# Attention scores of one head in one three-bank PSUM tile, with one maximum and one exponential

## The chip, the cores and the metric

The kernel runs on one core of a Trainium2 chip. The metric is the device time of one execution in microseconds (us). Each kernel is run several times, and the median is given. A difference of less than about 0.2% (7 us here) can't be told from no change.

## The reference

Two layers of a hybrid backbone run over 256 context tokens and 1024 latent tokens of width 1024. Each layer mixes the tokens by three groups of heads that share one input projection (attention, a gated recurrence in both directions, a Fourier transform), joins them by an output projection, and then applies a gated feed-forward part with a convolution. The change touches attention alone:

```python
def attend(q, k, v):
    s = jnp.einsum('bhgqd,bhkd->bhgqk', q, k).astype(jnp.float32) * (HEAD_DIM ** -0.5)
    p = jax.nn.softmax(s, axis=-1).astype(v.dtype)
    return jnp.einsum('bhgqk,bhkd->bhgqd', p, v)
```

There are 8 query heads of 64 channels and 2 key/value heads. A latent query sees all 1280 keys (256 of the context, 1024 latent), in both layers. A context query sees the 256 context keys, and is needed in layer 0 only.

## The kernel before, in words

**Tiles and units.** Queries go in tiles of 128 tokens: 2 of the context, 8 latent. A unit of `attention` is one tile and one pair of heads, so layer 0 has 8 units of the context and 32 latent ones, and layer 1 has 32 latent ones. In heads that is 16 of the context and 64 latent ones in layer 0, and 64 latent ones in layer 1: 144 in all.

**`score` (L545 to L590).** For each head of a unit the keys are cut into segments of at most 512, which gives 512, 512 and 256 for a latent head and one of 256 for a context head. Each segment has a PSUM tile of one bank, with the tag `s` and three buffers (L564). Two matmuls fill it (L566 and L567: queries against the low and high parts of the keys), VectorE takes its maximum over the keys (L569), and a second, small reduction joins the segments' maxima and negates them (L572). ScalarE then takes the exponential of each segment (L576) into an SBUF tile `p`, and adds up the rows into `su`. At a tile's last pair the sums are added over the segments (L584) and inverted (L585).

**`value` (L592 to L625).** For each two key blocks, TensorE transposes four 128x128 pieces of `p` into a one-bank tile `ps_t` (L602, two buffers), ScalarE copies out a rounded part `ph` (L607), VectorE the rest `pl` (L608), and four matmuls with the values add into `ps_o` (L612 and L614). A unit has five such steps for latent queries.

**PSUM.** While attention runs, the pool holds eight banks: three `s`, two `g` (projections, Fourier and others), one `o`, two `pt`.

**What sets the order.** L627 to L641 run the values of a unit in turns with the scores of the next one. `interleave` (L649) mixes attention with three other pieces of work, in this order: the rest of the input projection (`project_rest`: tiles `pxs` and `pws`, lines 158 to 160), the Fourier part, and the recurrence (tiles such as `psc`, `W`, `tot`). The table `LACE` holds the shares. A scheduler then orders each engine's instructions when the program is built, with its own estimates of durations; `ahead` (L107, table `AHEAD`) raises the priority of the named steps by a number per layer. On the chip each engine runs its instructions strictly in that order, and waits in it.

Of the kernel before, what the change touches and what calls it, by code (L numbers as in the profile page):

```python
# [11 lines left out]
F32 = mybir.dt.float32  # L12
# [47 lines left out]
QT_PAIRS = 1  # L60
QT_BUFS = 3
IN_WP = 2
P_BUFS = {512: 10, 256: 5}

C_Q, C_KV, C_HQ, C_HI, C_FF, C_FB, C_HG, C_FT = 0, 512, 768, 1024, 1280, 1536, 1792, 2048

# [30 lines left out]
def hybrid_backbone_kernel(ctx: ExitStack, tc: tile.TileContext, A: dict, out: bass.AP):  # L97
# [439 lines left out]
    def attention(l, S, ap, psn, finished):  # L537
# [6 lines left out]

        def score(i, pr):  # L545
            nk = keys(i)
            segs = [(s, min(512, nk * P - s)) for s in range(0, nk * P, 512)]
            ns = len(segs)
            if pr == 0:
                su = ap.tile([P, NH, 3], F32, tag="su", bufs=2, name="su")  # L550
                state["su", i] = su
            su = state["su", i]
            if pr % QT_PAIRS == 0:
                nh = 2 * QT_PAIRS
                state["qt"] = ap.tile([P, nh, P], F32R, tag="qt", bufs=QT_BUFS, name="qt")
                nc.gpsimd.dma_start(out=state["qt"], in_=S["QT"][i][:, 2 * pr:2 * pr + nh, :])  # L556
            qt = state["qt"]
            kv = pr // 2
            ps2 = []
            for h in (2 * pr, 2 * pr + 1):  # L560
                mx = ap.tile([P, 4], F32, tag="mx", bufs=4, name="mx")
                sc, p = [], []
                for j, (s0, n) in enumerate(segs):
                    t = psn.tile([P, 512], F32, tag="s", bufs=3, name="ps_s")  # L564
                    with ahead("qk" if (i, pr) != units[0] else "pt"):
                        nc.tensor.matmul(t[:, 0:n], lhsT=qt[:, h % (2 * QT_PAIRS), :], rhs=KT[:, 2 * kv + 1, s0:s0 + n], start=True, stop=False)  # L566
                        nc.tensor.matmul(t[:, 0:n], lhsT=qt[:, h % (2 * QT_PAIRS), :], rhs=KT[:, 2 * kv, s0:s0 + n], start=False, stop=True)  # L567
                    with ahead("max"):
                        nc.vector.tensor_reduce(out=mx[:, j:j + 1], in_=t[:, 0:n], axis=AX.X, op=ALU.max)  # L569
                    sc.append(t)  # L570
                with ahead("max"):
                    nc.vector.tensor_reduce(out=mx[:, 3:4], in_=mx[:, 0:ns], axis=AX.X, op=ALU.max, negate=True)  # L572
                for j, (s0, n) in enumerate(segs):
                    t = ap.tile([P, n], F32, tag=f"p{n}", bufs=P_BUFS[n], name="p")
                    with ahead("exp"):
                        nc.scalar.activation(out=t, in_=sc[j][:, 0:n], func=AF.Exp, bias=mx[:, 3:4],  # L576
                                             accum_out=su[:, h, j:j + 1])
                    p += [t[:, c:c + P] for c in range(0, n, P)]
                ps2.append(p)
                yield 0.84e-3 * nk * P  # L580
            state["p", i, pr] = ps2
            if pr == NH // 2 - 1:
                rs = ap.tile([P, NH], F32, tag="rs", bufs=2, name="rs")
                nc.vector.tensor_reduce(out=rs, in_=su[:, :, 0:ns], axis=AX.X, op=ALU.add)  # L584
                nc.vector.reciprocal(out=rs, in_=rs)  # L585
                t = psn.tile([P, 512], F32, tag="g", bufs=2, name="ps_rs")
                nc.tensor.transpose(t[0:NH, 0:P], in_=rs, identity=ident)
                rt = ap.tile([NH, P], F32, tag="rst", bufs=2, name="rst")
                nc.vector.tensor_copy(rt, t[0:NH, 0:P])
                nc.sync.dma_start(out=S["rs"][:, i * P:(i + 1) * P], in_=rt)  # L590
# [1226 lines left out]
```

## Time and profile before

| | us |
|---|---|
| median of 3 runs | 3408.84 |
| the runs | 3407.70 to 3414.72 |
| the profiled execution's own time | 3419.26 |
| its span, first to last instruction | 3417.4 |

The profile is of one execution. PE is TensorE's matmuls, PEld its loads of weights (the stationary operand), DVE is VectorE, ACT ScalarE, POOL GpSimd. The profiled execution is 10.4 us above the median, and 1.9 us of it lie outside the span. Attention runs from 284 to about 800 us in layer 0, and from 2060 to 2515 us in layer 1. In each layer it stands beside the input projection first (to about 500 and 2300 us), and beside Fourier and recurrence after that. A matmul's busy time in the profile is longer than the distance from its start to that of the next one, since they are pipelined.

### The profile page before, as it was taken

How to read it: one execution, taken by the hardware profiler on the slowest of the kernel's cores; microseconds unless marked ns; L12 is line 12 of the kernel's file. 1: busy time of each engine (PE TensorE's matmuls, PEld its weight loads, DVE VectorE, ACT ScalarE, POOL GpSimd, SP SyncE). 2: the span in 40 equal slices, each digit the busy share in tenths (PEclk: the TensorE clock that was granted, in tenths of full speed). 3: DMA queues.
4: the chain of work that ended last, by engine and by line, in shares of the span. 5: the costliest groups of instructions: out<-in, count | busy, mean ns of one | idle time of the engine just before them, and what ended most of it. 6: DMA issues, size and time to landing. Idle time of an engine off the chain costs nothing.

```text
span 3417.4 us, 55716 instructions
## 1 busy us (share of the span) xinstructions
PE 3116.8 (91%) x20897; PEld 2540.3 (74%) x20897; DVE 2417.0 (71%) x4171; ACT 1550.2 (45%) x3105; POOL 1261.6 (37%) x1134
## 2 busy tenths in 40 slices
PE   6999998989889999798899999998978889998896
PEld 4879976778766777576798888876766668776675
DVE  4614568887698888547876755668877798886568
ACT  4325556664443433233465435655642434443332
POOL 3522105422464444241235341115435545553323
PEclk9999999999989999899999999998998899999898
DMA  7643122117764443698775432122035642225993
GB/s 214 204 153 85 49 93 58 40 44 220 224 183 142 129 129 122 192 246 205 242 209 178 131 105 70 47 90 65 21 112 159 195 130 74 79 81 159 255 227 123
DMA packets 457412, 468.60 MB, mean 137 GB/s; under 512 B 32244, under 2 KB 343989, under 8 KB 457143
## 3 DMA queue, kind: packets, MB, share of 16 engines
q1 hardware_dynamic: 422294, 409.24, 37.9%
q0 software_dynamic: 34848, 55.80, 8.6%
q8 instruction: 165, 2.70, 0.3%
q14 instruction: 105, 0.85, 0.1%
HBM read 370.41 MB, written 94.54 MB: 136 GB/s over the span
## 4 chain that ended last, share of the span: by engine, by line
PE 28%; DVE 16%; DMA 14%; issue 9%; POOL 9%; ACT 3%; SPq 0%; POOLq 0%; DVEq 0%; ACTq 0%
PE pu L158 4%; POOL wlo L1217 4%; PE pu L159 4%; PE pu L160 4%; DMA araw<-act 3%; DMA X<-in_w_down_dram 3%; DVE cv L1105 3%; DMA raw<-in_w_down_dram 2%; PE ps_t L602 2%; PE ps_s L566 1%; DVE wlo L1348 1%; PE ps_o L612 1%; DVE U L1232 1%; DMA hraw<-yT 1%; DVE S L1204 1%
## 5 line engine op out<-in xcount | busy, mean ns | idle before, releaser
L1217 POOL TENSOR_TENSOR wlo<-S,whi 128x512 fp32r<-128x512 f32 x176 | 283.0, 1618 | 281.9 <-ACT whi L1216 268.2
L1105 DVE SCALAR_TENSOR_TENSOR cv<-U,cw,cv 128x512 f32<-128x512 f32 x352 | 326.0, 974 | 33.9 <-ACT cv L1102 33.8
L158 PE MATMUL pd<-whi,wlo 128*128 128x512 f32 x616 | 248.5, 411 | 58.5 <-DVE wlo L1348 50.2
L569 DVE TENSOR_REDUCE mx<-ps_s 128x1 f32<-128x512 f32 (+1 forms) x400 | 222.2, 588 | 108.0 <-PE ps_s L567 106.9
L608 DVE TENSOR_TENSOR pl<-ps_t,ph 128x512 fp32r<-128x512 f32 x328 | 223.0, 686 | 86.2 <-ACT ph L607 84.1
L145 POOL TENSOR_TENSOR wlo<-raw,whi 128x1024 fp32r<-128x1024 f32 x69 | 168.1, 2438 | 298.6 <-ACT whi L144 298.5
L602 PE MATMUL ps_t<-ident,p 128*128 128x128 f32 x1312 | 263.1, 284 | 13.6 <-DVE pl L608 8.1
L159 PE MATMUL pd<-wlo,whi 128*128 128x512 f32 x616 | 250.9, 407 | 17.5 <-DVE wlo L1348 14.3
L576 ACT ACTIVATE p<-ps_s,mx 128x512 f32<-128x512 f32 (+1 forms) x400 | 243.2, 617 | 52.0 <-DVE mx L572 42.3
L607 ACT CAST ph<-ps_t 128x512 fp32r<-128x512 f32 x328 | 190.9, 589 | 162.3 <-PE ps_o L614 80.4
L1102 ACT ACTIVATE cv<-U,cb,cw 128x512 f32<-128x512 f32 x176 | 137.6, 815 | 258.1 <-DVE U L1232 210.5
L160 PE MATMUL pd<-whi 128*128 128x512 f32 x616 | 249.2, 405 | 0.0
L158 PE MATMUL pxs<-whi,hlo 128*128 128x256 f32 x752 | 221.5, 295 | 5.8 <-DVE hraw L1524 4.3
L159 PE MATMUL pxs<-wlo,hhi 128*128 128x256 f32 x752 | 216.5, 288 | 0.5 <-DVE wlo L145 0.4
L160 PE MATMUL pxs<-whi,hhi 128*128 128x256 f32 x752 | 216.4, 288 | 0.0
L612 PE MATMUL ps_o<-pl,V 128*128 128x256 f32 x656 | 201.1, 323 | 6.7 <-DVE pl L608 4.8
L1217 POOL TENSOR_TENSOR wlo<-raw,whi 128x512 fp32r<-128x512 f32 x108 | 149.7, 1392 | 129.8 <-ACT whi L1216 115.6
L602 PEld LDWEIGHTS ps_t<-ident,p 128*128 128x128 f32 x1312 | 165.1, 143 | 36.8 <-DVE pl L608 10.9
L158 PEld LDWEIGHTS pd<-whi,wlo 128*128 128x128 f32 x616 | 119.3, 195 | 94.1 <-DVE wlo L1348 56.2
L1232 DVE TENSOR_TENSOR U<-pu,U 128x512 f32<-128x512 f32 x252 | 167.4, 686 | 26.9 <-PE pu L160 18.5
L614 PE MATMUL ps_o<-ph,V 128*128 128x256 f32 x656 | 183.2, 297 | 0.0
L556 POOL DMA_DIRECT2D qt<-QT x72 | 40.5, 563 | 374.6 <-PE ps_s L567 277.1
(395 smaller groups left out, 9423.6 us busy)
## 6 DMA issues: line engine op xcount, KB each, us to landing
raw<-in_w_up_dram SPq DMA_DIRECT2D x144, 512.0 KB
raw<-in_w_ada_dram SPq DMA_DIRECT2D x96, 512.0 KB
raw<-in_w_down_dram SPq DMA_DIRECT2D x62, 512.0 KB
act<-cv SPq DMA_DIRECT2D x88, 256.0 KB
araw<-act SPq DMA_DIRECT2D x40, 512.0 KB
raw<-in_w_in_dram SPq DMA_DIRECT2D x36, 512.0 KB
X<-in_w_down_dram POOLq DMA_DIRECT2D x30, 512.0 KB, 17.2
Y<-act POOLq DMA_DIRECT2D x30, 512.0 KB, 17.8
```

The costliest lines, as they stand in the source:

```text
L158: nc.tensor.matmul(o, lhsT=al, rhs=bh, start=start, stop=False)
L159: nc.tensor.matmul(o, lhsT=ah, rhs=bl, start=False, stop=False)
L160: nc.tensor.matmul(o, lhsT=ah, rhs=bh, start=False, stop=stop)
L569: nc.vector.tensor_reduce(out=mx[:, j:j + 1], in_=t[:, 0:n], axis=AX.X, op=ALU.max)
L576: nc.scalar.activation(out=t, in_=sc[j][:, 0:n], func=AF.Exp, bias=mx[:, 3:4], accum_out=su[:, h, j:j + 1])
L602: nc.tensor.transpose(t[:, ss, h, :], in_=ps2[h][2 * s2 + ss], identity=ident)
L607: nc.scalar.copy(ph, tv)
L608: nc.vector.tensor_tensor(out=pl, in0=tv, in1=f32(ph), op=ALU.subtract)
L612: nc.tensor.matmul(o, lhsT=V[:, s, kv, 1:3, :].rearrange("p a c -> p (a c)"), rhs=pl[:, ss, :], start=(s == 0), stop=False)
L1105: nc.vector.scalar_tensor_tensor(out=o, in0=u[:, tap:tap + n], scalar=convw[l][tap][:, c:c + 1], in1=o, op0=ALU.mult, op1=ALU.add)
L1217: nc.gpsimd.tensor_tensor(out=lo, in0=src, in1=f32(hi), op=ALU.subtract)
L1232: nc.vector.tensor_tensor(out=o, in0=x, in1=y, op=op)
```

## The change

A head's scores lie in one PSUM tile of three banks (1536 elements, of which 1280 or 256 are used), with one buffer. All six matmuls of a latent head write into it, each into a single bank. One reduction takes the negated maximum over all keys, and one exponential is written to a `p` tile of 1280 elements, of which there are five. The row sum comes from that exponential alone, so the small reductions of L572 and L584 are gone. PSUM use stays at eight banks, and the SBUF of `p` stays the same (10 x 512 + 5 x 256 = 5 x 1280). `LACE` and `AHEAD` stay as they were.

```diff
-P_BUFS = {512: 10, 256: 5}
+P_BUFS = 5
...
-                su = ap.tile([P, NH, 3], F32, tag="su", bufs=2, name="su")
+                su = ap.tile([P, NH], F32, tag="su", bufs=2, name="su")
...
-                mx = ap.tile([P, 4], F32, tag="mx", bufs=4, name="mx")
-                sc, p = [], []
-                for j, (s0, n) in enumerate(segs):
-                    t = psn.tile([P, 512], F32, tag="s", bufs=3, name="ps_s")
+                mx = ap.tile([P, 1], F32, tag="mx", bufs=4, name="mx")
+                t = psn.tile([P, 3 * 512], F32, tag="s", bufs=1, name="ps_s")
+                for s0 in range(0, n, 512):
+                    sl = slice(s0, min(n, s0 + 512))
                     with ahead("qk" if (i, pr) != units[0] else "pt"):
-                        nc.tensor.matmul(t[:, 0:n], lhsT=qt[:, h % (2 * QT_PAIRS), :], rhs=KT[:, 2 * kv + 1, s0:s0 + n], start=True, stop=False)
-                        nc.tensor.matmul(t[:, 0:n], lhsT=qt[:, h % (2 * QT_PAIRS), :], rhs=KT[:, 2 * kv, s0:s0 + n], start=False, stop=True)
-                    with ahead("max"):
-                        nc.vector.tensor_reduce(out=mx[:, j:j + 1], in_=t[:, 0:n], axis=AX.X, op=ALU.max)
-                    sc.append(t)
+                        nc.tensor.matmul(t[:, sl], lhsT=qt[:, h % (2 * QT_PAIRS), :], rhs=KT[:, 2 * kv + 1, sl], start=True, stop=False)
+                        nc.tensor.matmul(t[:, sl], lhsT=qt[:, h % (2 * QT_PAIRS), :], rhs=KT[:, 2 * kv, sl], start=False, stop=True)
                 with ahead("max"):
-                    nc.vector.tensor_reduce(out=mx[:, 3:4], in_=mx[:, 0:ns], axis=AX.X, op=ALU.max, negate=True)
-                for j, (s0, n) in enumerate(segs):
-                    t = ap.tile([P, n], F32, tag=f"p{n}", bufs=P_BUFS[n], name="p")
-                    with ahead("exp"):
-                        nc.scalar.activation(out=t, in_=sc[j][:, 0:n], func=AF.Exp, bias=mx[:, 3:4],
-                                             accum_out=su[:, h, j:j + 1])
-                    p += [t[:, c:c + P] for c in range(0, n, P)]
+                    nc.vector.tensor_reduce(out=mx, in_=t[:, 0:n], axis=AX.X, op=ALU.max, negate=True)
+                e = ap.tile([P, NT * P], F32, tag="p", bufs=P_BUFS, name="p")
+                with ahead("exp"):
+                    nc.scalar.activation(out=e[:, 0:n], in_=t[:, 0:n], func=AF.Exp, bias=mx, accum_out=su[:, h:h + 1])
+                p = [e[:, c:c + P] for c in range(0, n, P)]
...
-                nc.vector.tensor_reduce(out=rs, in_=su[:, :, 0:ns], axis=AX.X, op=ALU.add)
-                nc.vector.reciprocal(out=rs, in_=rs)
+                nc.vector.reciprocal(out=rs, in_=su)
```

The change also moves instructions, since the scheduler orders the whole program again. Outside the two attention stretches the order on TensorE is the same. In the changed kernel L566 and L567 are still the score matmuls and L569 is the maximum; the transposes are L596, the split L602, the value matmuls L606 and L608, the reciprocal L579, and `ob` L614.

On TensorE in layer 1, beside the input projection, the order before has this. A head's three score tiles (`ps_s`, six matmuls) are written as the banks come free, here the first one ahead of two value matmuls and the others behind them:

```order
9292 L612 MATMUL ps_o<-pl,V 128x256
9293 L614 MATMUL ps_o<-ph,V 128x256
9294 L566 MATMUL ps_s<-KT,qt 128x512
9295 L567 MATMUL ps_s<-KT,qt 128x512
9296 L612 MATMUL ps_o<-pl,V 128x256
9297 L614 MATMUL ps_o<-ph,V 128x256
9298 L566 MATMUL ps_s<-KT,qt 128x512
9299 L567 MATMUL ps_s<-KT,qt 128x512
9300 L566 MATMUL ps_s<-KT,qt 128x256
9301 L567 MATMUL ps_s<-KT,qt 128x256
9302 L612 MATMUL ps_o<-pl,V 128x256
```

In the order of the change the six stand together, and behind them come other matmuls up to the next head's six. The previous head's last score matmul here is number 9405; from 9406 to 9427 stand 9 value matmuls, 11 projection matmuls and 6 transposes, whose end is shown:

```order
9421 L158 MATMUL pxs<-whi,hlo_18244 128x256
9422 L159 MATMUL pxs<-wlo,hhi_18243 128x256
9423 L606 MATMUL ps_o<-pl,V 128x256
9424 L608 MATMUL ps_o<-ph,V 128x256
9425 L606 MATMUL ps_o<-pl,V 128x256
9426 L608 MATMUL ps_o<-ph,V 128x256
9427 L596 MATMUL ps_t<-ident,p 128x128 x2
9428 L566 MATMUL ps_s<-KT,qt 128x512
9429 L567 MATMUL ps_s<-KT,qt 128x512
9430 L566 MATMUL ps_s<-KT,qt 128x512
9431 L567 MATMUL ps_s<-KT,qt 128x512
9432 L566 MATMUL ps_s<-KT,qt 128x256
```

The score matmuls of a head moved together, and the distance to the next head's became one stretch of other work.

On VectorE at about the same place, the order before has the three maxima and the small one (`mx`) between the splits (`pl`):

```order
2224 L608 TENSOR_TENSOR pl<-ps_t,ph 128x512 x2
2225 L569 TENSOR_REDUCE mx<-ps_s 128x1 x3
2226 L608 TENSOR_TENSOR pl<-ps_t,ph 128x512
2227 L572 TENSOR_REDUCE mx<-mx 128x1
2228 L608 TENSOR_TENSOR pl<-ps_t,ph 128x512
2229 L589 COPY rst<-ps_rs 8x128
```

In the order of the change one reduction stands for the four, between two splits each time:

```order
2055 L602 TENSOR_TENSOR pl<-ps_t,ph 128x512 x2
2056 L569 TENSOR_REDUCE mx<-ps_s 128x1
2057 L602 TENSOR_TENSOR pl<-ps_t,ph 128x512
2058 L583 COPY rst<-ps_rs 8x128
2059 L602 TENSOR_TENSOR pl<-ps_t,ph 128x512
```

A split that could slip in between the maxima of a head now stands before or behind one longer reduction.

## Rows read from the trace of the kernel before

**Rows 1.** The page: each engine's busy time, share of the span and instructions.
```profile
PE 3116.8 (91%) x20897; PEld 2540.3 (74%) x20897; DVE 2417.0 (71%) x4171; ACT 1550.2 (45%) x3105; POOL 1261.6 (37%) x1134
```

**Rows 2.** Stretches: start:end, length, busy (x count) of PE, PEld, DVE, ACT, POOL; PEclk.
```profile
284.00:500.00 216.00, 212.59 (x1452) 186.69 (x1453) 123.93 (x289) 124.45 (x326) 26.77 (x30) 0.99 0.26 78
500.00:800.00 300.00, 272.88 (x3813) 222.40 (x3812) 239.81 (x584) 193.37 (x506) 112.32 (x155) 0.95 0.24 68
2060.00:2300.00 240.00, 237.78 (x1567) 201.67 (x1566) 145.16 (x303) 146.40 (x372) 30.74 (x35) 1.00 0.23 68
2300.00:2515.00 215.00, 192.48 (x2891) 156.83 (x2890) 174.14 (x410) 132.61 (x357) 88.34 (x112) 0.94 0.14 39
```

**Rows 3.** Stretches of the score tile alone: busy (x count) of PE, PEld, DVE, ACT.
```profile
500.00:800.00 300.00, 65.67 (x211) 35.01 (x210) 59.50 (x108) 71.90 (x216) 0.95 0.24 68
...
2300.00:2515.00 215.00, 43.00 (x144) 24.00 (x144) 41.36 (x72) 50.42 (x150) 0.94 0.14 39
```

**Rows 4.** Groups by line and shape, VectorE: count | busy, mean ns | idle before.
```profile
L608 DVE TENSOR_TENSOR pl<-ps_t,ph 128x512 fp32r<-128x512 f32 x328 | 223.0, 686 | 86.2 <-ACT ph L607 84.1
L569 DVE TENSOR_REDUCE mx<-ps_s 128x1 f32<-128x512 f32 x256 | 171.3, 685 | 76.2 <-PE ps_s L567 75.5
...
L569 DVE TENSOR_REDUCE mx<-ps_s 128x1 f32<-128x256 f32 x144 | 59.7, 416 | 31.8 <-PE ps_s L567 31.4
...
L572 DVE TENSOR_REDUCE mx<-mx 128x1 f32<-128x3 f32 x128 | 19.0, 149 | 1.2
```

**Rows 5.** Groups by line and shape, ScalarE, same columns.
```profile
L607 ACT CAST ph<-ps_t 128x512 fp32r<-128x512 f32 x328 | 190.9, 589 | 162.3 <-PE ps_o L614 80.4 <-PE ps_t L602 72.2 <-DVE pl L608 3.5
L576 ACT ACTIVATE p<-ps_s,mx 128x512 f32<-128x512 f32 x256 | 176.0, 692 | 39.5 <-DVE mx L572 38.6
...
L576 ACT ACTIVATION_READ_ACCUMULATOR p<-ps_s,mx 128x1 f32 x400 | 82.2, 206 | 0.0
L576 ACT ACTIVATE p<-ps_s,mx 128x256 f32<-128x256 f32 x144 | 69.3, 482 | 12.5 <-PE ps_t L602 8.3 <-DVE mx L572 3.7
```

**Rows 6.** Line L566 (first score matmul): its engine sat idle until (us, times).
```profile
  ACT p L576: 25.2, 88
```

**Rows 7.** Lines L602 (transposes) and L612 (first value matmul): idle until (us, times).
```profile
  DVE pl L608: 18.9, 22
...
  ACT p L576: 4.9, 12
...
  DVE pl L608: 13.4, 22
```

**Rows 8.** Timeline of TensorE in layer 1: start, us, line and operation, count.
```profile
2155.34 0.28 PE L612 MATMUL ps_o<-pl,V 128*128 128x256 f32 x1
2155.45 0.28 PE L614 MATMUL ps_o<-ph,V 128*128 128x256 f32 x1
...
2156.28 0.39 PE L566 MATMUL ps_s<-KT,qt 128*128 128x512 f32 x1
2156.51 0.39 PE L567 MATMUL ps_s<-KT,qt 128*128 128x512 f32 x1
...
2158.74 0.60 PE L602 MATMUL ps_t<-ident,p 128*128 128x128 f32 x4
2159.10 0.36 PE L158 MATMUL pxs<-whi,hlo 128*128 128x256 f32 x1
...
2331.85 0.76 PE L773 MATMUL psc<-q,kc 64*32 64x32 f32 x64
```

**Rows 9.** Timelines of VectorE and ScalarE in layer 0, one handover from maximum to exponential.
```profile
427.20 0.16 DVE L572 TENSOR_REDUCE mx<-mx 128x1 f32<-128x3 f32 x1
...
427.39 0.69 ACT L576 ACTIVATE p<-ps_s,mx 128x512 f32<-128x512 f32 x1 [2.48 <-DVE mx L572]
```

**Rows 10.** TensorE at attention's start: a timeline row [idle before], then a stretch 2 us later.
```profile
284.29 0.38 PE L566 MATMUL ps_s<-KT,qt 128*128 128x256 f32 x1 [2.39 <-DMA qt<-QT]
...
286.00:289.30 3.30, 3.30 (x18) 3.30 (x17) 0.61 (x3) 0.97 (x4) 0.11 (x1) 0.50 0.16 40
```

More of the change, by code (lines that the diff above doesn't have):

```diff
@@ L546, in score @@
             nk = keys(i)
-            segs = [(s, min(512, nk * P - s)) for s in range(0, nk * P, 512)]
-            ns = len(segs)
+            n = nk * P
             if pr == 0:
-                su = ap.tile([P, NH, 3], F32, tag="su", bufs=2, name="su")
+                su = ap.tile([P, NH], F32, tag="su", bufs=2, name="su")
                 state["su", i] = su
```

## The prediction, as put on record

> **What bounds the kernel now.** I read the page first: TensorE is busy for 91% of the span, VectorE for 71%, ScalarE for 45% [rows 1]. A mean over stages says little about a change that touches attention alone, so the second view is the busy time by stretch [rows 2]. Each layer's attention has two halves. Beside the input projection (284 to 500 and 2060 to 2300 us) TensorE is busy for 212.6 of 216 and 237.8 of 240 us at a granted clock of 0.99 and 1.00, while VectorE and ScalarE are at 57 to 61%. There TensorE sets the time, and relief of the others can give back at most the 3.4 + 2.2 us in which it is idle. Beside the Fourier part and the recurrence (500 to 800 and 2300 to 2515 us) TensorE is idle for 27.1 + 22.5 = 49.6 us, VectorE is at 80 and 81%, and the clock is 0.95 and 0.94. There both can matter. The third view is who waits for whom at the lines of the change: TensorE waits before a score matmul for an exponential 88 times, 25.2 us in all [rows 6], and before transposes and value matmuls for the split `pl` for 18.9 + 13.4 = 32.3 us [rows 7]. So the question is what TensorE will wait for, not how busy the others are.
>
> **Work removed.** On VectorE a latent head now costs two maxima of 685 ns, one of 416 and a small one of 149 [rows 4]: 1.94 us. From 256 to 512 elements a maximum grows by 269 ns, so 1.05 ns an element on a fixed 0.15 us; over 1280 elements that makes 1.49 us, 0.45 less. Over 128 latent heads this is 57 us of busy time; the context heads' small maxima (16 x 0.15) and the 18 sums of L584 add under 6 us. On ScalarE two exponentials of 692 ns, one of 482 and three accumulator reads of 206 [rows 5] make 2.48 us a head. One exponential over 1280, by the slope of 0.82 ns on a fixed 0.27 us, takes 1.32, and with one read 1.53: 0.95 less, 122 us in all. TensorE's work is the same: the same 800 score matmuls.
>
> What that relief is worth on the path: the 32.3 us of waits for `pl`. VectorE loses 57 of the 683 us that it is busy in the four stretches [rows 2], 8%; if the waits shrink as much, 3 us are gained. The lower bound is nothing, since a split that comes up behind a maximum now waits for up to 1.49 us, not 0.69; the upper bound is all 32 us. I take the 3: three quarters of a maximum's time remain, and it is in the way in larger pieces.
>
> **The wait added.** Before, the next head's first matmul needed one bank back: three maxima, the small one and the first exponential. Now it needs the whole tile back, and the one maximum can't start before the sixth matmul. From the last score matmul to the release lie 0.16 us (a matmul of 256 columns lasts 0.28 and the next starts 0.12 later [rows 8]), 1.49 for the maximum, a handover of 0.03 (427.36 to 427.39 [rows 9]), 1.32 for the exponential, and some 0.1 to TensorE: **3.1 us** with both engines free. Free they often aren't: half a split of 686 ns in front of the maximum and half a rounding of 589 ns in front of the exponential [rows 4, 5] add 0.64, so **3.7 us**; a whole one of each adds 1.28, so 4.4.
>
> Against it stands the other work that the new order puts between a head's sixth score matmul and the next head's first. I price it by the distances of starts: 0.115 us for 256 columns, 0.23 for 512, 0.09 to 0.10 for a transpose, 0.012 for a small matmul of the recurrence [rows 8]. The piece of order shown, 9 value matmuls, 11 of the projection and 6 transposes, is 20 x 0.115 + 6 x 0.10 = 2.9 us: 0.8 short of 3.7. Counted so over the whole order:
>
> - Beside the projection (66 gaps), 36 are shorter than 3.7 us, by 27.1 us in all; 20 are shorter than 3.1, by 9.7; 46 shorter than 4.4, by 55.5.
> - Beside Fourier and recurrence (36 and 24 latent heads [rows 3]), 57 of 60 are shorter than 3.7, by 67.2 us. But TensorE is idle there for 49.6 us anyway, waiting for others' chains, and that time passes in the gaps too: 67.2 - 49.6 = 17.6 us remain. At 3.1 the lack is 34.7, all of it covered; at 4.4 it is 107.2, so 57.6 remain.
> - The context heads need 0.16 + 0.42 + 0.03 + 0.48 = 1.1 us, and their 15 gaps lack 1.1 us of it in all (they had three buffers before).
>
> At 3.7 us this is 27.1 + 17.6 + 1.1 = 45.8 us, in place of the 25.2 us of the same wait now [rows 6]: **+20.6 us**. At 3.1 it is 10.8, so -14.4. I take 3.7 since the engines in front are busy for more than half of the time, and a mean of half an instruction is the nearest to that.
>
> **Smaller edits.** The transposes of a pair now wait for whole exponentials, where the first of them needed only the first 512 keys. TensorE waits there for 4.9 us in all [rows 7]; behind a head's exponential the order has the rest of the previous unit's values, which hides it, and without that cover each of 64 latent pairs would lose the other two exponentials' 0.69 + 0.48, up to 75 us. I cost it at nothing. `p` has five buffers of a head as before, and POOL's loads of `qt` are released by the same last score matmul. Nothing outside attention moves on TensorE.
>
> **Sum.** +20.6 - 3 = +17.6 us on the profiled execution, 3419.3 to 3436.9; it stands 10.4 us above the median of 3408.84, and on the median that is **3426 us**. A difference under 0.2%, 7 us, can't be told from none.
>
> **Rivals.**
>
> *Relief wins.* In the two recurrence halves VectorE is at 80%. If it is what the chains there wait for, the 60 heads there give back up to 60 x 0.45 = 27 us; half of it is 13. And if the release comes at 3.1 us, the score wait falls by 14.4. That makes 3408.8 - 13 - 14 = 3381, and 3395 if half of each holds; I put the middle at 3388. For it: 80% busy, and both engines' work falls by just what would stand in front of the maximum. Against it: in the projection halves there is next to nothing to regain. It decides where the release takes less than 3.2 us. The Trainium skill (Perfetto Trace Analysis, section "Optimizing Scalar/DVE Operations") says that larger operations help where VectorE or ScalarE is saturated, and that smaller ones can end work sooner where they aren't saturated but make others wait. By its first half this rival's time holds in the recurrence halves, by its second half the forecast in the others.
>
> *The banks no longer rotate.* If a whole split and a whole rounding stand in front, the release takes 4.4 us beside the projection: 55.5 + 17.6 + 1.1 - 25.2 = +49 us. Waits then pass 2 us, and such a wait has a price of its own: after the 2.39 us idle before the first score matmul, the granted clock was 0.50 from 286.0 to 289.3 us, half of full speed [rows 10], a loss of 1.65 us. Three gaps of 1.3 to 1.6 us would do that, 5 us. Together 3463. Against it: a stall lets the queues in front run empty, so the next gap is easier. The Trainium skill (the same page, section "Optimizing Tensor Performance") wants independent groups of matmuls to rotate through banks so that the evacuation of one overlaps the next. By that rule taken alone all 128 latent heads would pay the 3.7 us, +448 us less the 25.2, some 3830 us; the order shows 2 to 5 us of other matmuls in most gaps, so I give that extreme no chance of its own.
>
> *No difference.* The scheduler's gaps fit, the wait stays near 25 us, and the relief isn't on the path: 3409. For it: at 284 to 500 us 18 of 27 gaps are longer than 3.7 us. Against it: 39 gaps in layer 1's projection half lack 20.0 of the 27.1 us.
>
> **How the numbers follow.** The forecast (3416 to 3445) gets 0.44, rotation lost 0.11, no difference 0.18, relief 0.27. The signs follow: faster 0.27, same 0.18, slower 0.55. The range reaches from 3386, which leaves out some 0.12 of the relief rival, to 3455, which leaves out most of the second: 3386 to 3455. The forecast's own range is 3416 to 3445.
>
> **What would show it.** Right: one maximum near 1.49 us and one exponential near 1.32 on 128 heads; waits of the first score matmul for the exponential near 46 us, most of the growth between 2060 and 2300 us and in the recurrence halves; the projection halves longer. The step on the gaps is wrong if that wait stays near 25 us. The step on relief is wrong if the waits for `pl` fall by far more than 3 us, or if the recurrence halves get shorter. If the transposes wait for exponentials for over 15 us, the edit that I cost at nothing was not free.

## The result and the profile after

| | before | changed |
|---|---|---|
| median of four runs, us | 3411.09 | 3433.57 |
| the runs, us | 3407.70 to 3414.72 | 3431.79 to 3438.49 |
| ratio, 95% interval | | 1.0070 [1.0057, 1.0083] |
| the profiled execution's own time, us | 3419.26 | 3433.79 |

The changed kernel is slower by 22.5 us. Between the two profiled executions it is only 14.5 us, since the one of before lay some 8 us above its median and the one of after at its median. Whatever is read from the two traces has to be set against 14.3 us of span.

The page of the changed kernel, span and engines, against [rows 1]:

```profile
span 3431.7 us, 54849 instructions
...
PE 3125.8 (91%) x20897; PEld 2553.1 (74%) x20897; DVE 2383.8 (69%) x3753; ACT 1481.7 (43%) x2593; POOL 1262.7 (37%) x1134
```

VectorE has 418 instructions and 33 us less to do, ScalarE 512 instructions and 68 us less. TensorE has the same 20897 matmuls and is busy for 9.0 us longer. So 9.0 of the 14.3 us are the same matmuls taking longer, and 5.3 us are added idle time.

The groups by line and shape show that the new instructions cost what the prediction made of [rows 4, 5]: 1488 ns for the maximum (1.49 us) and 1333 for the exponential (1.32). Columns: count, then busy time and mean ns of one, then idle time before them and its releaser.

```profile
L602 DVE TENSOR_TENSOR pl<-ps_t,ph 128x512 fp32r<-128x512 f32 x328 | 222.2, 685 | 114.2 <-ACT ph L601 112.7
L569 DVE TENSOR_REDUCE mx<-ps_s 128x1 f32<-128x1280 f32 x128 | 190.4, 1488 | 93.8 <-PE ps_s L567 92.9
L572 ACT ACTIVATE p<-ps_s,mx 128x1280 f32<-128x1280 f32 x128 | 170.6, 1333 | 50.7 <-DVE mx L569 35.8 <-PE ps_t L596 14.4
```

Where does TensorE wait? First the idle time before the first score matmul, in the view of that line of the changed kernel (until what, us, times), then before the transposes, then before the first value matmul:

```profile
  ACT p L572: 25.1, 54
  issue: 3.2, 2
...
  DVE pl L602: 18.0, 40
  ACT p L572: 5.4, 11
...
  DVE pl L602: 37.8, 39
  DVE ob L614: 12.7, 15
```

The wait that was to grow from 25.2 to 45.8 us stands at 25.1: 54 waits in place of 88, each longer [rows 6]. The waits for the split `pl`, which were to shrink, have gone from 32.3 to 55.8 us [rows 7], and the wait for the bank of the values (until VectorE has copied out `ob`) has come up to 12.7. These views add the idle time of TensorE's two sequences, weight loads and matmuls, and the weight loads run ahead. The matmuls alone show what reaches the path. The same lines in the grouping of the changed kernel, matmuls only:

```profile
L596 PE MATMUL ps_t<-ident,p 128*128 128x128 f32 x1312 | 263.9, 289 | 9.3 <-DVE pl L602 5.3 <-ACT p L572 2.0 <-DVE fo L695 1.2
L606 PE MATMUL ps_o<-pl,V 128*128 128x256 f32 x656 | 202.3, 327 | 23.0 <-DVE pl L602 17.4 <-DVE ob L614 5.1
```

And the views of the same three lines of the kernel before, restricted to the matmuls: score matmul, transposes, value matmul:

```profile
  ACT p L576: 3.0, 8
...
  DVE pl L608: 8.1, 6
...
  DVE pl L608: 4.8, 7
...
  DVE ob L620: 0.5, 1
```

Of the 25.2 us of score wait only 3.0 were idle time of the matmuls; the other 22 are the weight loads', which wait while earlier matmuls can still run. After, it is 7.8 us by the same view; in three other orders of the kernel before (ctl_a, ctl_b and ctl_m5 below) it is 4.5 to 7.3, so this alone marks no lost buffer. The wait for `pl` before matmuls goes from 12.9 to 22.7 us.

Now the stretches, with the columns of [rows 2]. First the four of [rows 2] in the changed kernel, then each layer's attention from its first score matmul to the first matmul of the output projection (285.3 to 783.6 and 2087.5 to 2541.1 us), which holds the same work in every kernel here:

```profile
284.00:500.00 216.00, 208.16 (x1405) 180.17 (x1406) 110.29 (x175) 108.19 (x208) 26.17 (x29) 1.00 0.26 76
500.00:800.00 300.00, 271.12 (x3768) 223.57 (x3768) 228.55 (x450) 169.75 (x357) 110.16 (x149) 0.91 0.19 54
2060.00:2300.00 240.00, 236.46 (x1579) 207.23 (x1578) 128.71 (x179) 123.75 (x211) 31.45 (x31) 1.00 0.22 68
2300.00:2515.00 215.00, 193.22 (x2830) 153.91 (x2830) 163.35 (x319) 114.08 (x242) 88.08 (x116) 0.92 0.14 41
...
285.30:783.60 498.30, 462.88 (x5111) 390.60 (x5111) 326.27 (x601) 272.25 (x556) 132.74 (x174) 0.95 0.20 56
2087.50:2541.10 453.60, 418.18 (x4364) 351.79 (x4364) 303.97 (x526) 248.00 (x478) 117.31 (x146) 0.95 0.19 56
```

The kernel before, the same two stretches of work:

```profile
284.30:763.50 479.20, 449.37 (x5109) 380.68 (x5110) 336.49 (x818) 303.26 (x811) 131.91 (x174) 0.97 0.20 58
2075.90:2525.30 449.40, 416.85 (x4364) 346.48 (x4364) 325.41 (x727) 281.85 (x734) 116.98 (x146) 0.97 0.19 55
```

Attention is longer by 19.1 us in layer 0 and by 4.2 in layer 1. TensorE's idle time (length less busy time) has grown from 29.8 to 35.4 and from 32.6 to 35.4, by 8.5 us in all; its busy time has grown by 13.5 + 1.3 = 14.8, with a granted clock of 0.95 in place of 0.97. Of the 23.3 us 8.5 come back between layer 0's output projection and layer 1's first score matmul, where no line was changed: 1312.4 us before, 1303.9 after, and 1304.8 to 1317.9 in the traces of the twelve kernels below. That stretch scatters by some 10 us without any change to it.

The recurrence halves carry most of it. From the first matmul of the recurrence's small chains (`psc`) to the last `psc<-W,kc`, before:

```profile
527.00:732.00 205.00, 190.46 (x3259) 155.63 (x3260) 170.56 (x422) 138.47 (x380) 95.72 (x129) 0.94 0.13 35
2331.00:2484.00 153.00, 141.95 (x2474) 112.47 (x2474) 126.54 (x302) 98.44 (x270) 67.95 (x91) 0.97 0.11 29
```

and after:

```profile
532.50:749.60 217.10, 199.59 (x3243) 163.37 (x3244) 166.79 (x329) 122.17 (x263) 96.81 (x129) 0.89 0.13 32
2341.00:2500.50 159.50, 146.22 (x2480) 117.19 (x2479) 120.72 (x240) 88.67 (x193) 69.26 (x93) 0.93 0.10 28
```

They are longer by 12.1 and 6.5 us. Of these 18.6 us 5.2 are idle time, and 13.4 are busy time of about the same number of matmuls, at a granted clock of 0.89 and 0.93 in place of 0.94 and 0.97. Length times (1 - granted clock), an upper bound of what the lower clock can take away since it counts idle time too, goes from 12.3 + 4.6 to 23.9 + 11.2.

### The profile page after: what moved, and what is told of

It reads as the page before. It is cut to its first block, busy times and chain, and to the rows that moved or that the text cites. A ratio compares the mean times of both kernels' runs of the same rounds, so it can differ in the third digit from the quotient of the medians.

```text
span 3431.7 us, 54849 instructions
## 1 busy us (share of the span) xinstructions
PE 3125.8 (91%) x20897; PEld 2553.1 (74%) x20897; DVE 2383.8 (69%) x3753; ACT 1481.7 (43%) x2593; POOL 1262.7 (37%) x1134
## 4 chain that ended last, share of the span: by engine, by line
PE 26%; DVE 13%; DMA 11%; issue 9%; POOL 8%; ACT 2%; SPq 0%; POOLq 0%; DVEq 0%; ACTq 0%
POOL wlo L1211 4%; PE pu L158 3%; PE pu L159 3%; PE pu L160 3%; DMA araw<-act 3%; DMA X<-in_w_down_dram 2%; PE ps_t L596 2%; DVE cv L1099 2%; DMA Y<-act 2%; PE ps_s L566 1%; DVE wlo L1342 1%; PE ps_o L606 1%; PE ps_s L567 1%; PE pd L158 1%; PE pd L159 1%
## 5 line engine op out<-in xcount | busy, mean ns | idle before, releaser
L1099 DVE SCALAR_TENSOR_TENSOR cv<-U,cw,cv 128x512 f32<-128x512 f32 x352 | 327.8, 979 | 32.3 <-ACT cv L1096 32.1
L602 DVE TENSOR_TENSOR pl<-ps_t,ph 128x512 fp32r<-128x512 f32 x328 | 222.2, 685 | 114.2 <-ACT ph L601 112.7
L596 PE MATMUL ps_t<-ident,p 128*128 128x128 f32 x1312 | 263.9, 289 | 9.3 <-DVE pl L602 5.3
L569 DVE TENSOR_REDUCE mx<-ps_s 128x1 f32<-128x1280 f32 (+1 forms) x144 | 197.1, 1369 | 107.6 <-PE ps_s L567 106.6
L159 PE MATMUL pd<-wlo,whi 128*128 128x512 f32 x616 | 252.3, 410 | 16.6 <-DVE wlo L1342 15.2
L606 PE MATMUL ps_o<-pl,V 128*128 128x256 f32 x656 | 202.3, 327 | 23.0 <-DVE pl L602 17.4
L572 ACT ACTIVATE p<-ps_s,mx 128x1280 f32<-128x1280 f32 (+1 forms) x144 | 178.2, 1238 | 58.7 <-DVE mx L569 43.8
L596 PEld LDWEIGHTS ps_t<-ident,p 128*128 128x128 f32 x1312 | 164.4, 144 | 33.9 <-DVE pl L602 12.7
L158 PEld LDWEIGHTS pd<-whi,wlo 128*128 128x128 f32 x616 | 120.1, 196 | 88.4 <-DVE wlo L1342 48.2
L608 PE MATMUL ps_o<-ph,V 128*128 128x256 f32 x656 | 183.6, 299 | 0.0
```

What stands on the lines that cost most here:

```text
L158: nc.tensor.matmul(o, lhsT=al, rhs=bh, start=start, stop=False)
L159: nc.tensor.matmul(o, lhsT=ah, rhs=bl, start=False, stop=False)
L569: nc.vector.tensor_reduce(out=mx, in_=t[:, 0:n], axis=AX.X, op=ALU.max, negate=True)
L572: nc.scalar.activation(out=e[:, 0:n], in_=t[:, 0:n], func=AF.Exp, bias=mx, accum_out=su[:, h:h + 1])
L596: nc.tensor.transpose(t[:, ss, h, :], in_=ps2[h][2 * s2 + ss], identity=ident)
L602: nc.vector.tensor_tensor(out=pl, in0=tv, in1=f32(ph), op=ALU.subtract)
```

## The experiments

The prediction's theory was: one buffer makes TensorE wait (+20.6), fewer instructions give a little back (-3). The rivals after the result: both terms are much larger and cancel; or the scheduler's new order, and the clock that goes with it, makes the difference whatever the buffers. The table has all twelve runs. "Idle" is the length of the two attention stretches less TensorE's busy time in them, "busy" that busy time, each from one profiled execution.

| kernel | median, us | ratio to before, 95% | idle | busy |
|---|---|---|---|---|
| before | | 1 | 62.4 | 866.2 |
| m3e3: one tile, three maxima, three exponentials | 3458.27 | 1.0135 [1.0115, 1.0155] | 101.0 | 865.9 |
| m3: one tile, three maxima | 3448.62 | 1.0104 [1.0084, 1.0123] | 88.4 | 870.3 |
| e3: one tile, three exponentials | 3446.20 | 1.0105 [1.0086, 1.0124] | 85.4 | 870.8 |
| changed | 3433.57 | 1.0070 [1.0057, 1.0083] | 70.8 | 881.1 |
| p1280: before with one `p` tile a head | 3410.50 | 0.9996 [0.9983, 1.0008] | 59.0 | 860.7 |
| ctl_m5: before, priorities shifted by 5 | 3419.64 | 1.0018 [1.0006, 1.0030] | 70.8 | 860.1 |
| ctl_a: before, 5 the other way | 3436.72 | 1.0074 [1.0058, 1.0090] | 67.8 | 884.1 |
| ctl_b: before, score priorities lower | 3439.61 | 1.0080 [1.0066, 1.0094] | 73.1 | 882.0 |
| after_m5: changed, priorities of ctl_m5 | 3435.01 | 1.0067 [1.0054, 1.0080] | 79.1 | 869.9 |
| after_5: changed, priorities of ctl_a | 3442.74 | 1.0087 [1.0073, 1.0101] | 70.8 | 883.1 |
| split_first: changed, split first | 3429.95 | 1.0053 [1.0033, 1.0072] | 76.5 | 872.8 |
| exp_first: changed, exponential first | 3437.99 | 1.0080 [1.0064, 1.0096] | 72.0 | 878.5 |
| two_tiles: changed, tiles of two banks and one | 3432.37 | 1.0059 [1.0045, 1.0074] | 77.8 | 865.3 |

Two things stand out. Idle time goes with the kind of kernel: 59.0 to 73.1 us with three rotating banks, 70.8 to 79.1 in the five orders of the changed kernel, 85.4 to 101.0 with one tile and operations taken apart. Busy time does not: the same matmuls take 860 to 884 us in the orders of the kernel before and 870 to 883 in those of the changed one.

### The change in parts: m3e3, m3, e3

m3 keeps the changed kernel's tile and exponential, but takes the maximum bank by bank and joins the three:

```diff
-                    nc.vector.tensor_reduce(out=mx, in_=t[:, 0:n], axis=AX.X, op=ALU.max, negate=True)
+                    for j, s0 in enumerate(range(0, n, 512)):
+                        nc.vector.tensor_reduce(out=m4[:, j:j + 1], in_=t[:, s0:min(n, s0 + 512)], axis=AX.X, op=ALU.max)
+                    nc.vector.tensor_reduce(out=mx, in_=m4[:, 0:-(-n // 512)], axis=AX.X, op=ALU.max, negate=True)
```

> Edit: the changed kernel, but the maximum is taken over each bank again (three reductions and the small one), as soon as its two matmuls are done; one tile of three banks, one exponential. Theory of the long pieces (one maximum of 1.49 us stands in front of the splits, TensorE waits for the splits, idles, and its granted clock halves): the waits for the split fall from 56 us to under 40, and the time to 3411 to 3422, near the kernel before. Theory of the single buffer (the tile comes back late): the release is at most 0.4 us earlier, VectorE has 0.45 us a head more to do, so 3430 to 3445, as slow as the change or slower. Theory of chance (each new order of the scheduler meets another number of half-clock stretches): anywhere in 3400 to 3445, with the time following the clock lost in the two recurrence halves and not the waits.

e3 keeps the one maximum and takes the exponential bank by bank, with the sum over three partial sums at the end of a tile:

```diff
-                    nc.scalar.activation(out=e[:, 0:n], in_=t[:, 0:n], func=AF.Exp, bias=mx, accum_out=su[:, h:h + 1])
+                    for j, s0 in enumerate(range(0, n, 512)):
+                        sl = slice(s0, min(n, s0 + 512))
+                        nc.scalar.activation(out=e[:, sl], in_=t[:, sl], func=AF.Exp, bias=mx, accum_out=su[:, h, j:j + 1])
```

> Edit: the changed kernel, but the exponential is taken over each bank again (three instructions, three sums and their addition); one tile of three banks, one maximum. Theory of the long pieces: the long maximum stays in front of the splits, so 3428 to 3442. Theory of the single buffer: ScalarE needs 0.4 us more a head before the tile is free, so 3435 to 3455, slower than the change. Theory of chance: anywhere in 3400 to 3445.

m3e3 has both of these edits, so that against the kernel before only the tile (one of three banks in place of three of one), the grain of `p` and the scheduler's order differ:

> Edit: the changed kernel with three maxima, the small one and three exponentials, as before the change; all that is left of the change is that the three banks are one tile that comes back as a whole, and p one tile of 1280. Theory of the long pieces: 3411 to 3422, as little as the kernel before or a few us more. Theory of the single buffer: this alone carries the loss, so 3435 to 3460. Theory of chance: anywhere in 3400 to 3460.

The single tile without the merged operations costs 1.35%, 46 us, and in attention this is idle time. The two attention stretches of m3e3:

```profile
284.70:795.80 511.10, 457.29 (x5111) 389.38 (x5111) 342.07 (x819) 301.35 (x812) 133.70 (x174) 0.95 0.19 55
2107.30:2563.10 455.80, 408.56 (x4359) 348.94 (x4360) 315.46 (x725) 277.44 (x733) 115.10 (x146) 0.96 0.18 54
```

Attention takes 966.9 us in place of 928.6, and TensorE is busy for 865.9 in place of 866.2: all 38.3 us are idle time. Where the waits sit, by the views of the three lines (score matmul, transposes, first value matmul; both sequences of TensorE):

```profile
  ACT p L577: 28.3, 63
...
  ACT p L577: 20.2, 26
  DVE pl L608: 10.9, 18
...
  DVE pl L608: 26.0, 41
  DVE ob L620: 22.0, 12
  DVE mx L572: 10.5, 10
```

Here too the score wait itself is little above the 25.2 of before. The transposes wait for 20.2 us in place of 4.9 for exponentials, and the value matmuls for the bank of the values. Of the matmuls alone, the score wait is 8.9 us (3.0 before), the transposes' wait for exponentials 8.3 (1.6), and the wait for the values' bank 10.4 (0.5).

One tile is not only given back as a whole, it is also started on as a whole. In m3e3 and m3 no latent head's first maximum starts before its sixth score matmul is done, though the two matmuls of its own bank are done sooner; in the kernel before it does so in 118 of 128 latent heads, in the median 0.9 us earlier. One head of m3e3 in layer 1, its sixth matmul and its maxima (L571):

```profile
2149.93 0.28 PE L567 MATMUL ps_s<-KT,qt 128*128 128x256 f32 x1
2150.25 1.62 DVE L571 TENSOR_REDUCE m<-ps_s 128x1 f32<-128x512 f32 x3 [0.33 <-PE ps_s L567]
```

So the 46 us hold both losses, the rotation between heads and the overlap within a head; no run takes them apart. The edit of m3, a maximum as soon as its two matmuls are done, didn't have that effect.

From m3e3 one exponential (m3) or one maximum (e3) each gives back 0.3%, and both together 0.65%, 22 us: the steps add up. The prediction had 3. Each step is one order against one other, though, and smaller than the scatter of orders shown below. In the traces idle time falls from 101.0 to 88.4 and 85.4 and with both to 70.8, by 30.2 us, half of which is lost again to busy time (+15.2, at clocks of 0.95 and 0.95 in place of 0.95 and 0.96). The profiled executions of m3 and e3 lie 9.5 us below and 7.5 above their medians, so their rows in the table are rougher than those of m3e3 and of the changed kernel, which lie within 2 us.

e3 and m3e3 lie in the ranges of the single buffer's theory; m3 (3448.62) is above the range of every theory written down for it. Its waits for `pl` fell to 11.8 + 20.7 = 32.5 us, under the 40 that the theory of the long pieces asked for, and the time rose all the same, so that theory is out.

### The grain of `p`: p1280

The kernel before, with its three score tiles, but `p` as five tiles of 1280 elements:

```diff
-P_BUFS = {512: 10, 256: 5}
+P_BUFS = 5
...
+                e = ap.tile([P, NT * P], F32, tag="p", bufs=P_BUFS, name="p")
...
-                    t = ap.tile([P, n], F32, tag=f"p{n}", bufs=P_BUFS[n], name="p")
+                    t = e[:, s0:s0 + n]
```

> Edit: the kernel before, with three one-bank score tiles, three maxima and three exponentials, but p as one tile of 1280 with five buffers, as in the change. Theory of the single PSUM buffer: p's grain costs nothing, 3402 to 3416, within 0.2% of the kernel before. Rival, that p's grain carries the loss (a whole head's p comes back late, so exponentials wait for it): 3425 to 3455.

No difference: 0.9996 [0.9983, 1.0008]. So the 1.35% of m3e3 don't come from the grain of `p`.

### The order alone: ctl_a, ctl_m5, ctl_b, after_5, after_m5

The next question was how far the time moves when nothing but the scheduler's order moves. ctl_a is the kernel before with four priorities of `AHEAD` shifted by 5 (the rows of layers 0 and 1, first entries; the others stay):

```diff
-    {"qk": 50, "max": 100,
+    {"qk": 55, "max": 105,
...
-    {"qk": 150, "max": 50,
+    {"qk": 145, "max": 55,
```

> Edit: the kernel before, with four priorities moved by 5 (score matmuls 50 to 55 and 150 to 145, maxima 100 to 105 and 50 to 55). Nothing is bought by it: it measures how far another order alone moves the time. If orders are close to each other in worth: 3400 to 3418. If the order's chance makes the differences seen so far: some 20 us or more off the kernel before, 3428 or over.

ctl_m5 shifts them the other way (45 and 95, 155 and 45), ctl_b sets the score matmuls' to 40 and 120:

> Edit: the kernel before, with the same four priorities moved by 5 the other way (score matmuls 50 to 45 and 150 to 155, maxima 100 to 95 and 50 to 45). Theory that the kernel before sits on an order that happens to be good: 3425 to 3445, as the first shifted control. Theory that the first control was an unlucky order: 3404 to 3418.

> Edit: the kernel before, with the score matmuls' priorities lowered further (50 to 40, 150 to 120). Theory that the kernel before sits on an order that happens to be good: 3425 to 3450. Theory that the first control was an unlucky order: 3404 to 3420.

The kernel before has 1.0018, 1.0074 and 1.0080 of its own time in these orders. Two of the three moves are as large as the whole effect of the change. ctl_a's recurrence half in layer 0 looks just like that of the changed kernel, in length and in clock, with three banks that rotate:

```profile
530.70:748.00 217.30, 198.86 (x3258) 162.58 (x3258) 168.35 (x419) 137.58 (x380) 94.89 (x128) 0.89 0.12 33
```

Over attention its idle time is 67.8 us, 5.4 more than before, and its busy time 17.9 us more. So a lower clock in the recurrence isn't a mark of the single buffer.

The changed kernel was then given the same two pairs of priorities, for a comparison at equal ones:

> Edit: the changed kernel, with the priorities of the first control (55, 145, 105, 55). Theory that the change's loss is the order alone: its neighbours scatter around the shifted kernels before, 3405 to 3445, and some lie below 3420. Theory that the single buffer costs by itself what the larger instructions don't give back: 3428 to 3460, above the shifted kernels before, by some 20 us on the mean.

> Edit: the changed kernel, with the priorities of the second control (45, 155, 95, 45). Theory that the change's loss is the order alone: 3405 to 3445, with no distance to the shifted kernels before on the mean. Theory that the single buffer costs by itself what the larger instructions don't give back: 3428 to 3460.

At equal priorities the changed kernel stands against the one before at +0.70% (as found), +0.13% (ctl_a's, intervals overlap) and +0.49% (ctl_m5's). The mean of the three is 0.44%, 15 us. Every one is on the slower side, but how much of the 22.5 us belongs to the change, and how much to the order in which the kernel before happens to be written, three pairs don't settle. Over all orders measured, four of the kernel before and five of the changed one, the means (1.0043 and 1.0071) differ by 0.28%, 10 us. The times of after_5 and after_m5 lie in the ranges of both theories, so they don't decide between them.

The cost of the single tile is above this scatter, as far as one order of m3e3 can tell. m3e3 (at least 1.0115) is slower than all four orders of the kernel before (at most 1.0094) and than all five of the changed one (at most 1.0101).

### Priorities for the changed kernel: split_first, exp_first

If a large maximum in front of the split makes TensorE wait, then the split should go first. split_first sets the priority of "split" in both layers from 0 to 150, exp_first that of "exp" from 0 to 100:

```diff
-    {"qk": 50, "max": 100, "exp": 0, "pt": 50, "split": 0,
+    {"qk": 50, "max": 100, "exp": 0, "pt": 50, "split": 150,
...
-    {"qk": 150, "max": 50, "exp": 0, "pt": 30, "split": 0,
+    {"qk": 150, "max": 50, "exp": 0, "pt": 30, "split": 150,
```

> Edit: the changed kernel, with the priority of the split (ScalarE's ph and VectorE's pl) raised by 150 in both layers, so that the scheduler puts it in front of a maximum that it now stands behind. Theory of the long pieces: the waits for the split fall from 56 us to under 40, those for the score tile rise by some 10 us, and the time comes to 3412 to 3428. Theory of the single buffer: the maximum comes later and the tile back later, so 3435 to 3455. Theory of chance: anywhere in 3400 to 3445.

> Edit: the changed kernel, with the priority of the exponential raised by 100 in both layers, so that on ScalarE it goes ahead of the roundings ph and the tile comes back earlier. Theory of the single buffer: the waits for the tile fall below 20 us, and the time by 3 to 12 us, to 3420 to 3430, unless the delayed roundings take it back. Theory of the long pieces: the roundings and splits come later still, so 3435 to 3450.

split_first's waits at the score matmul, the transposes and the first value matmul, both sequences:

```profile
  ACT p L572: 17.2, 47
...
  DVE pl L602: 29.7, 53
...
  DVE pl L602: 25.6, 40
  DVE ob L614: 17.7, 12
```

The wait for `pl` is 55.3 us in place of 55.8: it only moved from the value matmuls to the transposes. The score wait fell by 7.9, the wait for the values' bank rose by 5.0. The time, 1.0053 [1.0033, 1.0072], can't be told from the changed kernel's, so this edit doesn't test what a shorter wait would give. exp_first, 1.0080, gains nothing either: its score wait is 26.6 us, not the under 20 that it was made for.

### Between the two: two_tiles

Keys 0 to 1023 in a tile of two banks, the rest in one of a single bank, with a maximum and an exponential for each:

```diff
+                segs = [(0, 1024, "sA"), (1024, n, "sB")] if n > 1024 else [(0, n, "sB")]
...
+                    t = psn.tile([P, 1024 if tg == "sA" else 512], F32, tag=tg, bufs=1, name="ps_s")
...
+                    for j, (a0, a1, tg) in enumerate(segs):
+                        nc.scalar.activation(out=e[:, a0:a1], in_=sc[j][:, 0:a1 - a0], func=AF.Exp, bias=mx, accum_out=su[:, h, j:j + 1])
```

> Edit: the changed kernel with a head's scores in two tiles, one of two banks (1024 keys) and one of one bank (256 keys), each with one buffer; a maximum and an exponential for each, the small maximum and the sum of two. It gives back a third of the rotation and takes back about half of the saved work. Theory of the single buffer (the whole tile's return is what costs, the larger instructions save): between the change and the kernel before if rotation by two pieces is worth more than the work, 3415 to 3432; as slow as the kernels with one maximum or one exponential taken apart if it isn't, 3436 to 3450. Theory of chance: anywhere in 3400 to 3450.

1.0059 [1.0045, 1.0074]: not resolved from the changed kernel, slower than before, and at the edge of the range (3415 to 3432) in which rotation by two pieces was worth the work. Its score wait is the longest of all, 35.3 us over both sequences. No version tried beats the kernel before; p1280 is level with it.

## Why the prediction came out as it did

The direction was right, and 3433.57 lies in the forecast's own range. The sum was +17.6 us; measured are +22.5. The way there was not the one predicted, so that the number fits is in good part luck.

- **Durations: right.** 1.49 and 1.32 us forecast, 1.488 and 1.333 measured.
- **The wait added (+20.6): mis-sized, and in another place.** The single tile costs 46 us by m3e3. The step on the gaps, that the lack of each gap appears as a wait of the next score matmul, is what failed, by the mark set for it: this wait stays at 25.1 us, and at 28.3 even where the buffer costs 46. It began from the wrong number as well: of the 25.2 us of before only 3.0 were idle time of the matmuls (and of the 32.3 of waits for `pl` 12.9). In m3e3 the cost appears at later steps of the chain: transposes waiting for exponentials (20.2 us), value matmuls for the values' bank (22.0). Why there is not shown; the likely reason is that the scheduler orders all engines anew for the new tile.
- **The projection halves (a lack of 27.1): nothing of it in layer 1.** From the first score matmul to the last matmul of the projection's rest, layer 0 takes 170.1 us in place of 165.3, layer 1 176.9 in place of 177.4. For most heads the 3.7 us were too long here. In the changed kernel's trace, a latent head takes 3.17 us at least from the start of its sixth score matmul to the end of the exponential, in the median 3.20 and 3.47 us in the two projection halves and 3.87 and 4.24 in the recurrence halves. 31 of the 55 heads in the projection halves take less than 3.4 us: there the engines were as good as free, the case for which the prediction had counted a lack of 9.7.
- **The context heads (1.1): too small.** TensorE's idle time from 284 to 500 us grew from 3.4 to 7.8 us [rows 2], and 2.5 of these 4.4 us fall into the 40 us in which the context heads run (285 to 325 us: busy for 39.85 us before, 37.33 after); about 1 us of the 4.4 is only that attention starts 1.1 us later. The score matmuls wait there for 2.3 us for exponentials (6.6 with the weight loads), and not at all before. This cost comes with the change in every order read: TensorE is idle for 2.5, 2.5 and 4.1 us in that half in the changed kernel's (as found, after_5, after_m5), for 0.4, 1.0 and 0.2 in those of before (as found, ctl_a, ctl_m5).
- **The recurrence halves (17.6 of lack): the size right, the reason not.** They are longer by 12.1 + 6.5 us. By the rows above, idle time grew by 5.2 us in them, and the same work took 13.4 us more of busy time at the lower clock. The prediction counted a lower clock only for the rival. Whether the lower clock comes of the new waits or of the order itself stays open: no run held the clock up.
- **Relief (-3): mis-sized, seven times too small as far as one order each shows.** One maximum and one exponential give back 22 us together. The Trainium skill (Perfetto Trace Analysis, section "Optimizing Scalar/DVE Operations") ties the gain of larger operations to a saturated engine. In m3e3's attention in layer 0 VectorE is busy for 342 of 511 us and ScalarE for 301, 67 and 59%, and each of the two still gained 0.3%. So the step that took the gain as 8% of a wait was the wrong measure: from the sixth score matmul's start to the last exponential's end a latent head takes 5.06 us in the mean in m3e3 and 4.14 in the changed kernel, and with a single buffer the next head waits for that end. That this is what the time went by is argued, not shown. By the mark on relief (waits for `pl` falling by far more than 3 us) it would have looked right: they rose, and yet the time fell from m3e3 to the changed kernel.
- **Free edits: right.** The grain of `p` costs nothing (p1280), and in the changed kernel the transposes wait 5.4 us for exponentials, against 4.9.
- **The rivals.** "Banks no longer rotate" comes close in price, +49 us there and 46 measured for the single tile, but not in place: it put its 49 us into the score wait, which m3e3 raises by 3. The Trainium skill's rule on rotating banks (Perfetto Trace Analysis, section "Optimizing Tensor Performance") agrees in its sign; the 448 us of it taken alone don't occur (the prediction's 3830 us for it takes the 25.2 off twice: 3409 + 448 is 3857). "Relief wins" has the right sign for its part and falls short, 22 us against 46, and its place isn't borne out: the recurrence halves, first to last matmul of `psc`, get no shorter from m3e3 to the changed kernel. Their idle time falls by 13.6 us, and their busy time rises by 18.1 at a lower clock. m3e3 first, then the changed kernel:

```profile
542.30:769.00 226.70, 197.46 (x3380) 164.37 (x3381) 181.25 (x445) 141.79 (x395) 99.93 (x132) 0.92 0.12 32
2368.40:2536.90 168.50, 151.04 (x2646) 125.51 (x2646) 133.74 (x328) 106.48 (x295) 70.62 (x95) 0.95 0.10 26
...
532.80:759.30 226.50, 207.96 (x3368) 169.44 (x3369) 175.49 (x346) 126.75 (x272) 99.36 (x132) 0.89 0.12 31
2341.30:2514.50 173.20, 158.62 (x2648) 128.28 (x2648) 132.75 (x266) 94.87 (x206) 72.22 (x96) 0.93 0.09 25
```

- **Luck.** The two errors of the sum, 25 and 19 us, nearly cancelled.

What is shown: one tile of three banks costs idle time of TensorE, and the merged operations give back less than that. What isn't: that the net is 22.5 us in other orders (10 to 15 us by the means above), what the two parts cost in other orders, and how far the lower clock follows from either.

## What to carry to other kernels

Where TensorE sets the pace, banks that rotate can be worth more than the instruction overhead that a merged operation saves (46 against 22 us here): take the two apart (buffer without merging) before keeping or dropping both. In a kernel whose order a scheduler makes, a lost buffer need not appear as a wait for that buffer; compare the idle and the busy time of TensorE over the whole stage of equal work, matmuls apart from weight loads. And shift priorities by a trifle to learn the scatter of orders before a difference under 1% is given a cause.

## What the runs showed that was not expected

The granted clock can stay at half for long after a short stall, or not fall at all after a longer one. At the start of attention it was 0.50 for 3.3 us after an idle time of 2.39 us [rows 10]. The same matmul of the changed kernel stands behind an idle time of 2.40 us, and there the clock stays at 1.00, so the price that the second rival put on such a wait isn't a fixed one:

```profile
285.35 0.36 PE L566 MATMUL ps_s<-KT,qt 128*128 128x256 f32 x1 [2.40 <-DMA qt<-QT]
...
284.00:294.00 10.00, 8.61 (x67) 8.14 (x68) 2.39 (x5) 3.90 (x13) 1.06 (x2) 1.00 0.40 113
```

In the changed kernel's recurrence, TensorE had two shorter idle times, in the timeline of its matmuls:

```profile
657.06 0.54 PE L767 MATMUL psc<-W,kc 64*32 64x32 f32 x32 [1.17 <-DVE rst L583]
658.11 0.39 PE L606 MATMUL ps_o<-pl,V 128*128 128x256 f32 x1 [0.52 <-DVE pl L602]
```

VectorE in front of them, in its timeline: a maximum of 1.49 us, and behind it the copy and the split that the profile names as what TensorE waited for.

```profile
654.88 1.49 DVE L569 TENSOR_REDUCE mx<-ps_s 128x1 f32<-128x1280 f32 x1
...
656.72 0.28 DVE L583 COPY rst<-ps_rs 8x128 f32<-8x128 f32 x1
...
657.38 0.68 DVE L602 TENSOR_TENSOR pl<-ps_t,ph 128x512 fp32r<-128x512 f32 x1
```

The stretches that follow, columns as in [rows 2]:

```profile
656.00:660.00 4.00, 2.42 (x45) 1.64 (x45) 3.87 (x10) 2.71 (x6) 1.14 (x2) 0.93 0.03 7
660.00:664.00 4.00, 4.00 (x24) 2.59 (x26) 1.09 (x3) 0.59 (x1) 0.30 (x1) 0.50 0.00 0
...
676.00:680.00 4.00, 4.00 (x22) 3.65 (x21) 2.01 (x6) 2.44 (x6) 0.74 (x1) 0.52 0.00 0
680.00:684.00 4.00, 4.00 (x34) 3.80 (x33) 2.63 (x4) 1.79 (x6) 1.85 (x3) 1.00 0.10 22
```

From 660 to 680 us the clock is at the lower of its two levels, 1.2 GHz, although TensorE is busy for all of that time; this takes away some 10 us. The kernel before has such stretches in this half as well: in steps of 4 us, three with a lowered clock, of 12, 12 and 8 us, where the changed kernel has four, of 16, 12, 24 and 8. That the idle times in front lowered the clock fits the rows but isn't shown by a run. If they did, a stall's price isn't read from its length.
